# Products of a chunked recurrence grouped by the shape of their weights, and an order whose estimate counts changes of shape

## The chip, the cores and the metric

The kernel runs on one core of a Trainium2 chip. Its engines are TensorE (PE, with the weight loads listed apart as PEld), VectorE (DVE), ScalarE (ACT), GpSimd (POOL) and SyncE (SP, which only issues DMAs). The metric is the device time of one execution in microseconds, lower is better; the figure is the median of several executions.

## The reference

Two decoder layers and a final norm, for 256 prompt rows and 8 sample rows that share the weights. Each layer is a feed-forward half step, a mixer, and another feed-forward half step. The mixer of layer 0 joins a gated delta net (four heads) and differential attention (four heads); that of layer 1 is latent attention. The change touches the gated delta net of the prompt, which the reference computes in chunks of 64 rows:

```python
    def step(S, xs):
        q_i, k_i, u_i, w_i, a_i, gl = xs
        v_new = u_i - jnp.einsum('bhck,bhkv->bhcv', w_i, S)
        o = jnp.einsum('bhck,bhkv->bhcv', q_i, S) + jnp.einsum('bhij,bhjv->bhiv', a_i, v_new)
        S = S * jnp.exp(gl)[..., None, None] + jnp.einsum('bhck,bhcv->bhkv', k_i, v_new)
        return S, o
```

Here `u` and `w` are the solutions of a triangular system of each chunk, found before the scan. The eight samples make one step of the same recurrence each, from states of 256 KB that come from memory.

## The kernel before

All activations lie with features on the partitions and the 264 rows (prompt and samples together) as columns. A projection is a stream of 128 x 128 weight blocks: each block is split into a high and a low part (`whl`, by ACT and DVE), and three products of 264 columns use it. Small float32 products run as two passes, so a product of `mm` is two MATMUL records in the trace; the projection's products are one record each.

The program is written as threads (generators): `proj` is the mixer's input projection, `gdn` the recurrence of the prompt, `gdn_s` the step of the samples, `diff_p`, `diff_s` and `diff_v` the differential attention (`diff_s` multiplies the gathered keys `dk`, `diff_v` the gathered values `dv`), `post_d` and `post_g` the norms of the heads and the output projection (products on `mix`). A class `Clock` merges them into one queue for each engine: `emit` takes the instruction with the earliest estimated start, and `cost` holds the estimated durations. Nothing is reordered afterwards: the queues are fixed when the program is built, each engine works its own off in order, and the estimate only decides who stands before whom. A part written under `clk.group()` is placed as one piece. Where the estimate sees PE idle, `keep_warm` puts in products of a constant that nobody reads (`ps_pe<-busy`), so that the clock stays up; in the text they are called fillers.

What stands around the change in the mixer of layer 0:

- `gdn` inverts the triangular matrices by doubling (ten products `ps_pd<-ya` and `ps_pd<-yb,ya` of 64 x 64 blocks, sixteen at a time), transposes the keys, and then makes, for each half `b` of the heads' rows, `up` (weights of 64 rows and 64 columns) and `wpp` (weights of 64 rows and 128 columns), one product of each in turn.
- The scan has four chunks. A chunk makes `vp` from the state `SS`, on DVE the new values `vn`, then `sp` (the state's update) and `op_` (the output). `op_` of each head accumulates two products: one with the state as weights (128 rows), one with `vn` as weights (64 rows), again in turn.
- `gdn_s` waits for `proj`: the tiles `xh` and `xl`, which hold the projection's input, receive the samples' states. For four samples at a time it multiplies the states by keys and queries (`xh,gsw`, then `xl,gsw`), works on DVE, and adds the update (`gsr`).
- `post_g` waits for `gdn`, `gdn_s` and `proj`. So the first product on `mix` comes after the longer of the two recurrences and a head norm.

The accumulators are slots: `pa` two, `pc` one, `pd` three banks. `W.limit` holds the splitting of the output projection's weights back until `post_g` calls `W.resume()`.

Of the kernel before, what the change touches and what calls it, by code (L numbers as in the profile page):

```python
# [14 lines left out]
AF = mybir.ActivationFunctionType  # L15
# [127 lines left out]
class Virtual:  # L143
    """A tile whose place is chosen when its first instruction is put into a queue."""
# [5 lines left out]
class Slots:  # L150
    """Places of one shape for virtual tiles. The place of a tile is free again when its thread has gone past the
    segment that made it (keep: when the thread has called free) and its last instruction is in a queue."""
# [35 lines left out]
class Clock:  # L188
    """Puts the instructions that the threads create into the engine queues in the order of their
    estimated starts, so that no queue waits long at its head."""  # L190
# [5 lines left out]
    def __init__(self):  # L196
        self.free, self.reg, self.prev, self.rings = {}, {}, {}, {}
        self.pipe = self.hw = 0.0
        self.columns = {}
        self.spare = None  # L200
        self.seq = 0
        self.cur = self.atom = None
        self.waiting = {}
        self.done = {}
        self.virtual, self.segment = [None], []

    # -- tiles
# [48 lines left out]
    def when(self, r, write, eng=None):  # L256
        """When an instruction of `eng` may use the region."""
# [32 lines left out]
    # -- cost estimates  # L290
# [17 lines left out]
    def cost(self, eng, name, out, ins, k):  # L308
        n = max([self.size(out)] + [self.size(i) for i in ins]) if eng == "DVE" else self.size(out)
        if eng == "PE":  # L310
# [4 lines left out]
            if ins[0].dtype == F32R:  # L315
                return max(2.5 + n * 0.4167, m * 0.8333), n, share
# [21 lines left out]
    # -- instructions  # L338
# [82 lines left out]

    def start(self, eng, ri, ro):
        t = self.free.get(eng, 0.0)
        for r in ri:
            t = max(t, self.when(r, False, eng))
        for r in ro:
            t = max(t, self.when(r, True, eng))
        return t

    def pe(self, t, c, cols, share):  # L430
        """The tensor engine's clock is halved in each tick after one in which few columns left the array."""
# [6 lines left out]
    def keep_warm(self, t):  # L438
        """Matmuls that nobody reads, up to time t."""
        while self.spare:  # L440
# [3 lines left out]
            if f + c > t - self.MARGIN:  # L444
                return
            self.spare()
            self.free["PE"] = self.pe(f, 109.0, 256, 1.0)

    def emit(self, op):
# [3 lines left out]
        if eng == "PE":  # L453
            self.keep_warm(self.start(eng, op.calls[0][6], op.calls[0][7]))
        for f, name, a, k, out, ins, ri, ro in op.calls:
# [36 lines left out]
    def add(self, name):  # L492
        """What the current thread has created so far makes `name` available."""
# [6 lines left out]
    # -- threads: generators that yield None (go on when all that they issued is done), a time, or the  # L500
    # names they wait for
# [53 lines left out]
def hybrid_trunk_kernel(ctx: ExitStack, tc: tile.TileContext, wall, xT, wba, vecs, cst0, cst1, ident_d, convst,  # L555
# [29 lines left out]
    def service(thread, f, *a):  # L585
        """f's instructions in a thread of their own, which nobody waits for as a whole."""
        cur = clk.cur
        clk.cur = cur and thread
        f(*a)
        clk.cur = cur  # L590

    # ------------------------------------------------------------ weight stream
    class Stream:
        """The weights, 128 x 128 blocks in the order of their use; units of 16 blocks are loaded, pieces of 4 split into
        a high and a low part, except those that raw() hands out whole."""
# [54 lines left out]
        def whole(self, use):  # L650
            """use(the next block); with float32 products for these there is nothing to split."""
# [13 lines left out]
    # in the tensor engine's gaps it multiplies a constant, so that its clock stays up  # L665
# [17 lines left out]
    def rsqrt(src, w, np_=128):  # L683
        """1/sqrt of a small tile on the vector engine."""
# [17 lines left out]
    # ------------------------------------------------------------ constants  # L702
# [30 lines left out]
    # ------------------------------------------------------------ norm statistics  # L733
# [88 lines left out]
    # ------------------------------------------------------------ driver  # L822
# [21 lines left out]
    def lead(xh, xl, tags):  # L844
        """The first blocks of a projection; the last rows of x come latest, so the first two blocks alternate."""
# [17 lines left out]
    # ------------------------------------------------------------ FFN  # L863
# [58 lines left out]
    # ------------------------------------------------------------ final norm  # L922
# [18 lines left out]
    def finish_y():  # L941
        """The statistics with the tokens on the partitions; a product with their diagonal spreads them."""
# [21 lines left out]
    # ------------------------------------------------------------ KV gather  # L964
# [5 lines left out]
    class Loader:  # L970
        """Gathers tiles of 32-row strips of four pages each, in order, into whichever slots are free."""
# [40 lines left out]
        def retire(self, tags):  # L1012
            """These slots are not filled again."""
# [8 lines left out]
    # ------------------------------------------------------------ one sample's softmax over its past  # L1022
    def scores(b, w, load, parts, SM, ready, cc, P, pT):
        """w [128, sub, 32]: the queries, one diagonal block for each page of a strip; parts: for each part
        of the features, its four strips' tiles. Leaves exponentials (strip, page, query row; key) in P,
        transposed in pT; returns the inverses of their sums."""
# [30 lines left out]
    def weigh(o, pT, load, strips, vs, dv):  # L1057
        """o [32 j + query row, dv]: the values weighed by pT."""
# [13 lines left out]
    # ============================================================ start  # L1072
# [69 lines left out]
    # ============================================================ layer 0 mixer  # L1142
    def mixer0():
        with tc.tile_pool(name="m0", bufs=1) as mp_:
# [16 lines left out]
            # ---- input projection  # L1161
# [70 lines left out]
            # ---- normalisation of four head blocks by their partition sums  # L1232
# [13 lines left out]
            # ---- gated delta net  # L1246
# [19 lines left out]
            def gdn():  # L1266
# [59 lines left out]
                # decay in (key, query) layout, 64-token chunks stacked two high  # L1326
# [12 lines left out]
                # Gram products  # L1339
# [60 lines left out]
                # token-major keys and values  # L1400
                KB, KE = [], []
                for b in range(2):
# [7 lines left out]
                    yield  # L1410
                for b in range(2):
                    up, wpp = ps("pd"), (ps("pd"), ps("pd"))
                    for h in range(4):
                        for r in range(2):
                            rr = slice(r * 64, r * 64 + 64)
                            uc = U[rr, (4 * b + h) * 64:(4 * b + h) * 64 + 64]
                            hc = slice(h * 128, h * 128 + 128)
                            mm(up[rr, hc], uc, VB[b][rr, hc], start=True, stop=True)
                            mm(wpp[r][:, h * 64:h * 64 + 64], KB[b][rr, hc], uc, start=True, stop=True)
                    S.activation(VB[b], up, AF.Copy)  # L1420
                    for r in range(2):
                        S.activation(KB[b].rearrange("p (h r t) -> p h r t", h=4, r=2)[:, :, r, :],
                                     wpp[r][:, 0:256].rearrange("p (h t) -> p h t", h=4), AF.Copy)
                    yield
                # scan over the chunks
# [3 lines left out]
                for c in range(4):  # L1429
                    b, r = divmod(c, 2)  # L1430
                    rr = slice(r * 64, r * 64 + 64)
                    vp = ps("pd")
                    for h in range(4):
                        hc = slice(h * 128, h * 128 + 128)
                        mm(vp[rr, hc], KB[b][:, h * 128 + r * 64:h * 128 + r * 64 + 64], SS[:, h, :], start=True, stop=True)
                    V.tensor_tensor(vn[rr, :], VB[b][rr, :], vp[rr, :], OP.subtract)
                    yield
                    op_, sp = ps("pd"), ps("pd")
                    tc0 = b * 128 + r * 64
                    for h in range(4):  # L1440
                        hc = slice(h * 128, h * 128 + 128)
                        mm(sp[:, hc], KE[b][rr, hc], vn[rr, hc], start=True, stop=True)
                    for h in range(4):
                        hc = slice(h * 128, h * 128 + 128)
                        oc = slice(h * 64, h * 64 + 64)
                        mm(op_[:, oc], SS[:, h, :], Q0[:, h, tc0:tc0 + 64], start=True, stop=False)
                        mm(op_[:, oc], vn[rr, hc], AT[rr, (4 * b + h) * 64:(4 * b + h) * 64 + 64], start=False, stop=True)
                    V.tensor_tensor(SS, SS, egl[:, r, 4 * b:4 * b + 4, None].to_broadcast([128, 4, 128]), OP.mult)
                    V.tensor_tensor(SS, SS, v3(sp, 4), OP.add)
                    S.activation(Q0[:, :, tc0:tc0 + 64], op_[:, 0:256].rearrange("p (h t) -> p h t", h=4), AF.Copy)  # L1450
# [4 lines left out]
            # ---- gated delta net, one step of each sample: four samples at a time, row 32 j + 4 i + h  # L1455
# [758 lines left out]
```

## Time and profile before

| | before |
|---|---|
| median of 3 executions | 1348.65 us (1345.4 to 1349.91) |
| span of the profiled execution | 1297.2 us |
| median less the span | 51.45 us |
| PE busy, share of the span | 1274.9 us, 98% |
| mean granted clock of TensorE | 0.979 |
| input projection of the layer 0 mixer | 205.3 to 386.2 us |
| from its last product to the first on `mix` | 386.2 to 487.9 us |

The profile is of one execution; its own time outside the profiler is not given, so its span is set beside the median. PE counts as busy from the start of a product to its modelled end, and products overlap, so 98% does not mean that PE does useful work at its peak: half-speed products and fillers count too.

### The profile page before, as it was taken

Reading aid. Unit: us, or ns where it says so; the run is one execution under the profiler, and the core shown is the slowest. Engines: PE = TensorE matmul, PEld = TensorE weight load, DVE = VectorE, ACT = ScalarE, POOL = GpSimd, SP = SyncE. Lnnn points to the kernel's source line nnn. Section 1 sums busy time; section 2 is a strip of 40 time slices with the busy share of each in tenths; the row PEclk is TensorE's granted clock in tenths of the full one; section 3 lists DMA queues with packets and bytes.
Section 4 is the critical chain, followed back from the end, with each engine's and each line's share of the span. In section 5 each row is a group of like instructions: output and inputs, shape, how many; then the busy total and the mean of one; then the engine's idle time right before and its main releaser. Section 6 shows DMA issues by size and latency. Waiting matters only on the chain.

```text
span 1297.2 us, 28444 instructions
## 1 busy us (share of the span) xinstructions
PE 1274.9 (98%) x11569; PEld 1146.7 (88%) x11569; DVE 874.0 (67%) x1855; ACT 580.7 (45%) x1185; POOL 433.4 (33%) x526
## 2 busy tenths in 40 slices
PE   9999999999999999999999999999999999999997
PEld 7999999967676567999999999999876679999996
DVE  6777667687762767877766777766874449777652
ACT  5555544345411024555554555544432235555541
POOL 3643222355552412553422222212334523322221
PEclk9999999999996879999999999999999999999999
DMA  7776556898897563676755454555467955555551
GB/s 286 264 272 233 192 168 229 285 342 320 304 344 288 167 229 133 230 282 221 260 167 192 163 194 168 191 171 187 161 240 278 393 166 176 191 181 178 195 167 63
DMA packets 52163, 287.72 MB, mean 222 GB/s; under 512 B 6192, under 2 KB 6768, under 8 KB 27200
## 3 DMA queue, kind: packets, MB, share of 16 engines
q1 hardware_dynamic: 28912, 180.77, 40.0%
q0 software_dynamic: 23120, 105.13, 22.3%
q8 instruction: 91, 1.49, 0.4%
q14 instruction: 40, 0.33, 0.1%
HBM read 280.95 MB, written 5.03 MB: 220 GB/s over the span
## 4 chain that ended last, share of the span: by engine, by line
PE 86%; DVE 5%; DMA 3%; issue 2%; ACT 1%; POOL 1%; SPq 0%; POOLq 0%; ACTq 0%; DVEq 0%
PE ps_pd L457 40%; PE ps_pa L457 37%; PE ps_pc L457 5%; PE ps_po L457 3%; DVE whl L457 2%; PE ps_pe L666 2%; DMA dv<-in_vpool_dram,pt 2%; DMA raw<-in_wall_dram 1%; ACT whl L457 0%; DVE wxl L457 0%; DMA x<-in_xT_dram 0%; DVE QW L457 0%; DVE x L457 0%; POOL t L457 0%; DVE QR L457 0%
## 5 line engine op out<-in xcount | busy, mean ns | idle before, releaser
L457 DVE TENSOR_TENSOR whl<-raw,whl 128x512 fp32r<-128x512 f32 x642 | 486.0, 766 | 214.7 <-ACT whl L457 208.3
L457 ACT ACTIVATE whl<-raw 128x512 fp32r<-128x512 f32 x642 | 399.8, 630 | 371.9 <-PE ps_pa L457 195.9
L457 PE MATMUL ps_pa<-wxh,whl 128*128 128x264 f32 x1616 | 325.0, 286 | 1.8 <-ACT t L457 0.8
L457 PEld LDWEIGHTS ps_pa<-wxh,whl 128*128 128x128 f32 x1616 | 260.8, 188 | 11.0 <-issue 6.6
L457 PE MATMUL ps_pd<-wxh,whl 128*128 128x264 f32 x1152 | 233.9, 285 | 0.0
L457 PE MATMUL ps_pa<-wxl,whl 128*128 128x264 f32 x808 | 231.1, 286 | 0.0
L457 PEld LDWEIGHTS ps_pd<-wxh,whl 128*128 128x128 f32 x1152 | 187.6, 188 | 0.9 <-DVE whl L457 0.4
L457 POOL TENSOR_TENSOR t<-t,t 128x264 f32<-128x264 f32 (+1 forms) x100 | 83.1, 831 | 275.6 <-DVE t L457 275.4
L457 PE MATMUL ps_pd<-wxl,whl 128*128 128x264 f32 x576 | 164.1, 285 | 0.0
L457 PEld LDWEIGHTS ps_pa<-wxl,whl 128*128 128x128 f32 x808 | 151.8, 188 | 4.9 <-issue 4.5
L457 PE MATMUL ps_pd<-ah,whl 128*128 128x264 f32 x704 | 130.9, 284 | 0.0
L457 PE MATMUL ps_pa<-ah,whl 128*128 128x264 f32 x704 | 130.7, 284 | 0.0
L457 PEld LDWEIGHTS ps_pd<-ah,whl 128*128 128x128 f32 x704 | 110.0, 188 | 0.0
L457 PEld LDWEIGHTS ps_pa<-ah,whl 128*128 128x128 f32 x704 | 109.9, 188 | 0.0
L457 PEld LDWEIGHTS ps_pd<-wxl,whl 128*128 128x128 f32 x576 | 108.2, 188 | 0.8 <-issue 0.8
L457 PE MATMUL ps_pd<-al,whl 128*128 128x264 f32 x352 | 99.9, 284 | 0.0
L457 PE MATMUL ps_pa<-al,whl 128*128 128x264 f32 x352 | 99.7, 283 | 0.0
L457 POOL TENSOR_TENSOR al<-t,ah 128x264 fp32r<-128x264 f32 x88 | 76.9, 874 | 58.0 <-ACT ah L457 57.9
L457 POOL TENSOR_TENSOR t<-x 128x264 f32<-128x264 f32 x45 | 32.8, 730 | 189.0 <-DVE x L457 183.3
L457 POOL DMA_INDIRECT dk<-in_kpool_dram,ptk x57 | 58.8, 1031 | 56.9 <-PE ps_pc L457 45.2
L457 PE MATMUL ps_pd<-wya,whl 128*128 128x264 f32 x352 | 71.2, 284 | 0.0
L457 PE MATMUL ps_pa<-wya,whl 128*128 128x264 f32 x352 | 71.0, 284 | 0.0
(414 smaller groups left out, 1964.6 us busy)
## 6 DMA issues: line engine op xcount, KB each, us to landing
raw<-in_wall_dram SPq DMA_DIRECT2D x162, 1024.0 KB, 4.9
out_y_dram<-wya SPq DMA_DIRECT2D x4, 264.0 KB, 2.6
xh<-in_rec_dram SPq DMA_DIRECT2D x4, 256.0 KB, 9.5
xl<-in_rec_dram SPq DMA_DIRECT2D x4, 256.0 KB, 17.6
out_recs_dram<-xh SPq DMA_DIRECT2D x4, 256.0 KB, 7.1
out_recs_dram<-xl SPq DMA_DIRECT2D x4, 256.0 KB, 4.3
dk<-in_kpool_dram,ptk POOLq DMA_INDIRECT x57, 6.3
cst<-in_cst_dram SPq DMA_DIRECT2D x1, 838.5 KB, 8.7
```

Source lines behind the costliest of these rows:

```text
L457: f(*a, **k)
L666: clk.spare = lambda: nc.tensor.matmul(pe[0:32, 0:256], busy[:, 0:32], busy, start=True, stop=True)
```

## The change

Four edits. (1) `up` and `wpp` are two loops instead of one: for both halves all products of `up` first, then all of `wpp`, each half's eight in one group. (2) In a chunk of the scan the four products of one kind form a group: `vp`, then the output's part from the state, then `sp`, then the part from `vn`. The two parts of the output no longer accumulate in one bank: ACT copies the first to `Q0`, the second goes into the bank of `vp`, and DVE adds it (one more DVE instruction in each chunk). A chunk has one `yield` instead of two, and it asks for its three `pd` banks at once. (3) `emit` adds `SWITCH`, 120 ns, to the estimated time of PE where the shape of the weights (rows and columns, each rounded up to 32, 64 or 128) differs from that of the product before. (4) `cost` takes 121 ns instead of 112.5 for a projection product of 264 columns. Comments and docstrings are blanked as well.

```diff
-                return max(2.5 + n * 0.4167, m * 0.8333), n, share
+                return max(11.0 + n * 0.4167, 5.0 + m * 0.8333), n, share
...
+    SWITCH = 120.0
+    @staticmethod
+    def shape(call):
+        return tuple(32 if n <= 32 else 64 if n <= 64 else 128 for n in (call[5][0].shape[0], call[4].shape[0]))
...
             self.keep_warm(self.start(eng, op.calls[0][6], op.calls[0][7]))
+            kind = self.shape(op.calls[0])
+            if kind != self.kind and "PE" in self.free:
+                self.free["PE"] += self.SWITCH
+            self.kind = self.shape(op.calls[-1])
...
+                def both(b, f):
+                    with clk.group():
+                        for h in range(4):
+                            for r in range(2):
+                                rr = slice(r * 64, r * 64 + 64)
+                                f(h, r, rr, slice(h * 128, h * 128 + 128), U[rr, (4 * b + h) * 64:(4 * b + h) * 64 + 64])
...
-                            mm(up[rr, hc], uc, VB[b][rr, hc], start=True, stop=True)
-                            mm(wpp[r][:, h * 64:h * 64 + 64], KB[b][rr, hc], uc, start=True, stop=True)
+                    up = ps("pd")
+                    both(b, lambda h, r, rr, hc, uc: mm(up[rr, hc], uc, VB[b][rr, hc], start=True, stop=True))
                     S.activation(VB[b], up, AF.Copy)
+                for b in range(2):
+                    wpp = ps("pd"), ps("pd")
+                    both(b, lambda h, r, rr, hc, uc: mm(wpp[r][:, h * 64:h * 64 + 64], KB[b][rr, hc], uc, start=True, stop=True))
...
-                        mm(op_[:, oc], SS[:, h, :], Q0[:, h, tc0:tc0 + 64], start=True, stop=False)
-                        mm(op_[:, oc], vn[rr, hc], AT[rr, (4 * b + h) * 64:(4 * b + h) * 64 + 64], start=False, stop=True)
+                    with clk.group():
+                        for h, _, o in hs:
+                            mm(o, SS[:, h, :], Q0[:, h, tc0:tc0 + 64], start=True, stop=True)
                     V.tensor_tensor(vn[rr, :], VB[b][rr, :], vp[rr, :], OP.subtract)
+                    q = Q0[:, :, tc0:tc0 + 64]
+                    S.activation(q, op_[:, 0:256].rearrange("p (h t) -> p h t", h=4), AF.Copy)
                     V.tensor_tensor(SS, SS, egl[:, r, 4 * b:4 * b + 4, None].to_broadcast([128, 4, 128]), OP.mult)
+                    with clk.group():
+                        for _, hc, _ in hs:
+                            mm(sp[:, hc], KE[b][rr, hc], vn[rr, hc], start=True, stop=True)
                     V.tensor_tensor(SS, SS, v3(sp, 4), OP.add)
-                    S.activation(Q0[:, :, tc0:tc0 + 64], op_[:, 0:256].rearrange("p (h t) -> p h t", h=4), AF.Copy)
+                    with clk.group():
+                        for h, hc, _ in hs:
+                            mm(vp[:, h * 64:h * 64 + 64], vn[rr, hc], AT[rr, (4 * b + h) * 64:(4 * b + h) * 64 + 64], start=True, stop=True)
+                    V.tensor_tensor(q, q, vp[:, 0:256].rearrange("p (h t) -> p h t", h=4), OP.add)
```

The queues change in nearly every part of the program, since the estimate runs differently from the first product on. Three places on PE matter here. The first is the start of the first half's `up` (`yb 64x128`) and `wpp` (`yb,ya 128x64`) before; `dk,QW` are key products of the samples, and a shape is that of the result.

```order
L457 MATMUL ps_pc_71<-dk,QW 32x128 x24
L457 MATMUL ps_pd_73<-yb 64x128
L457 MATMUL ps_pd_72<-yb,ya 128x64
L457 MATMUL ps_pd_73<-yb 64x128
L457 MATMUL ps_pd_74<-yb,ya 128x64
L457 MATMUL ps_pd_73<-yb 64x128
L457 MATMUL ps_pd_72<-yb,ya 128x64
```

The pattern goes on for 16 products, and for 16 more of the second half. The same place now, with what follows it on PE:

```order
L470 MATMUL ps_pa_69<-wxl,whl 128x264
L470 MATMUL ps_pd_74<-yb 64x128 x8
L470 MATMUL ps_pd_72<-yb 64x128 x8
L470 MATMUL ps_pd_73<-yb,ya 128x64
L470 MATMUL ps_pd_74<-yb,ya 128x64
L470 MATMUL ps_pd_73<-yb,ya 128x64
L470 MATMUL ps_pd_74<-yb,ya 128x64
```

The sixteen products of `up` stand together, then those of `wpp`, which alternate between two banks, and products of the input projection (`wxl,whl`) now stand ahead of them. The second place is a chunk of the scan: before, the first chunk's `sp` (`yb,ya 128x128`) and `op_` (`S,SS` and `yb 128x64` in turn), with a group of the samples' queries between.

```order
L457 MATMUL ps_pd_72<-yb,ya 128x128 x4
L457 MATMUL ps_pd_73<-S_3172,SS 128x64
L457 MATMUL ps_pd_74<-xh,gsw 32x512 x4
L457 MATMUL ps_pd_73<-yb 128x64
L457 MATMUL ps_pd_73<-S_3172,SS 128x64
L457 MATMUL ps_pd_73<-yb 128x64
L457 MATMUL ps_pd_73<-S_3172,SS 128x64
```

Now, from the first chunk's `vp` (`SS,ya`) to the second chunk's `sp`:

```order
L470 MATMUL ps_pd_74<-SS,ya 64x128 x4
L470 MATMUL ps_pd_72<-S_3163,SS 128x64 x4
L470 MATMUL ps_po<-dv,PT_2540 8x512 x4
L470 MATMUL ps_pd_73<-yb,ya 128x128 x4
L470 MATMUL ps_pd_74<-yb 128x64 x4
L470 MATMUL ps_pa_69<-wxh,whl 128x264 x2
L470 MATMUL ps_pa_69<-wxl,whl 128x264
L470 MATMUL ps_pa_69<-wxh,whl 128x264
L470 MATMUL ps_pd_72<-SS,ya 64x128 x4
L470 MATMUL ps_pd_73<-S_3163,SS 128x64 x4
L470 MATMUL ps_pd_74<-yb,ya 128x128 x4
```

Each kind stands in fours, the step of the samples is gone from between, and the projection is still being fed: the scan, which stood wholly behind the projection's last product, now stands wholly ahead of it. The third place is what follows that last product. Before, the first of these rows stand right behind it: fillers, the first of the inverse's last two stages and the samples' first small product (`mfs,ones`):

```order
L666 LDWEIGHTS busy
L666 MATMUL ps_pe<-busy 32x256
L457 MATMUL ps_pd_74<-ya 64x64 x16
L666 LDWEIGHTS busy
L666 MATMUL ps_pe<-busy 32x256
L457 MATMUL ps_pd_73<-mfs,ones 128x64
```

Now, after 18 fillers, it is two value strips (`dv`) and the step of the samples, and behind `xh,gsw` come 39 fillers in a row:

```order
L470 MATMUL ps_po<-dv,PT_2538 8x512 x4
L470 MATMUL ps_pd_72<-mfs,ones 128x64
L470 MATMUL ps_po<-MX,PT_2538 8x128 x4
L470 MATMUL ps_po<-dv,PT_2538 8x512 x4
L679 LDWEIGHTS busy
L679 MATMUL ps_pe<-busy 32x256
```

```order
L470 MATMUL ps_pd_73<-ones,t_77 128x1 x2
L470 MATMUL ps_pd_74<-ident,gsw 128x128 x4
L470 MATMUL ps_pd_72<-ob,cst_104 32x128 x4
L470 MATMUL ps_pd_73<-xh,gsw 32x512 x4
L470 MATMUL ps_pd_72<-xh,gsw 32x512 x4
L679 LDWEIGHTS busy
```

Nothing of the prompt's recurrence is left behind the last projection product. In the whole program the fillers go from 317 to 398: while the input projection runs from 48 to 33, between its last product and the first on `mix` from 83 to 189, among the first products on `mix` from 23 to 35, elsewhere from 163 to 141.

## Rows read from the trace of the kernel before

**Rows 1.** The page: busy time, granted clock in 40 slices, the chain's shares.
```profile
PE 1274.9 (98%) x11569; PEld 1146.7 (88%) x11569; DVE 874.0 (67%) x1855; ACT 580.7 (45%) x1185; POOL 433.4 (33%) x526
...
PEclk9999999999996879999999999999999999999999
...
PE 86%; DVE 5%; DMA 3%; issue 2%; ACT 1%; POOL 1%; SPq 0%; POOLq 0%; ACTq 0%; DVEq 0%
```

**Rows 2.** Busy time by stage; at the end granted clock, DMA share, GB/s.
```profile
205.30:386.20 180.90, 177.22 (x2184) 141.08 (x2182) 132.78 (x369) 72.75 (x179) 81.91 (x118) 1.00 0.86 309
386.20:487.90 101.70, 100.32 (x835) 60.03 (x833) 53.98 (x154) 15.41 (x42) 28.21 (x30) 0.78 0.65 237
487.90:520.30 32.40, 31.65 (x249) 26.49 (x248) 26.20 (x62) 13.86 (x27) 9.32 (x11) 1.00 0.32 113
520.30:909.30 389.00, 388.47 (x3181) 386.23 (x3180) 275.41 (x465) 203.31 (x373) 120.22 (x135) 1.00 0.58 202
```

**Rows 3.** PE in order of time around the projection's end: start, duration, instruction.
```profile
386.09 0.28 PE L457 MATMUL ps_pa<-wxh,whl 128*128 128x264 f32 x1
...
386.73 1.15 PE L457 MATMUL ps_pd<-ya 64*64 64x64 f32 x32
...
388.43 0.61 PE L666 MATMUL ps_pe<-busy 128*32 128x256 bf16 x4
...
391.21 1.04 PE L457 MATMUL ps_po<-dv,PT 128*8 128x512 f32 x8 [1.09 <-DMA dv<-in_vpool_dram,pt]
392.19 0.66 PE L457 MATMUL ps_pd<-ident,S 128*128 128x128 f32 x4
```

**Rows 4.** The same view, from 395 us: `up` and `wpp` in turn.
```profile
395.93 1.52 PE L457 MATMUL ps_pc<-dk,QW 128*32 128x128 f32 x48
397.38 0.43 PE L457 MATMUL ps_pd<-yb 64*64 64x128 f32 x2
397.74 0.43 PE L457 MATMUL ps_pd<-yb,ya 64*128 64x64 f32 x2
...
404.77 2.36 PE L457 MATMUL ps_pc<-dk,QW 128*32 128x128 f32 x40
407.06 0.69 PE L457 MATMUL ps_pd<-yb 64*64 64x128 f32 x2
...
416.88 1.51 PE L457 MATMUL ps_pc<-dk,QW 128*32 128x128 f32 x24
418.15 1.08 PE L457 MATMUL ps_pd<-xh,gsw 128*32 128x512 f32 x4
```

**Rows 5.** A stretch within these, columns as in group 2.
```profile
400.80:421.30 20.50, 20.50 (x124) 13.18 (x124) 0.91 (x3) 2.51 (x6) 4.29 (x5) 0.50 0.59 221
```

**Rows 6.** PE in order of time, the scan's last chunk.
```profile
462.23 1.16 PE L457 MATMUL ps_pd<-yb,ya 64*128 64x128 f32 x8
463.31 0.43 PE L457 MATMUL ps_pd<-S,SS 128*128 128x64 f32 x2
463.68 0.43 PE L457 MATMUL ps_pd<-yb 64*128 64x64 f32 x2
...
466.60 1.93 PE L457 MATMUL ps_pc<-dk,QW 128*32 128x128 f32 x32
```

**Rows 7.** Instructions on `xh`, 380 to 460 us: the last line.
```profile
DMA to landing us min/median/max: 7.0/7.4/11.2
```

**Rows 8.** DVE in order of time: the samples' step, the scan's end, the norm.
```profile
425.64 1.51 DVE L457 SCALAR_TENSOR_TENSOR t<-ps_pd,ghe,t 128x128 f32<-128x128 f32 x4 [2.06 <-PE ps_pd L457]
...
435.94 0.17 DVE L457 COPY S<-ps_pd 128x16 f32<-128x16 f32 x1
...
457.98 0.17 DVE L457 COPY S<-ps_pd 128x16 f32<-128x16 f32 x1 [0.66 <-PE ps_pd L457]
...
466.81 0.69 DVE L457 TENSOR_TENSOR SS<-SS,ps_pd 128x512 f32<-128x512 f32 x1
```

**Rows 9.** PE in order of time: the first products on `mix`.
```profile
487.92 0.39 PE L457 MATMUL ps_pa<-mix,whl 128*128 128x264 f32 x1
```

More of the change, by code (lines that the diff above doesn't have):

```diff
@@ L202, in __init__ @@
         self.cur = self.atom = None
+        self.kind = None
         self.waiting = {}
@@ L445, in keep_warm @@
                 return
+            self.kind = (128, 32)
             self.spare()
@@ L1410, in gdn @@
                     yield
-                for b in range(2):
[L1412 to L1417, printed above, removed]
-                            mm(up[rr, hc], uc, VB[b][rr, hc], start=True, stop=True)
-                            mm(wpp[r][:, h * 64:h * 64 + 64], KB[b][rr, hc], uc, start=True, stop=True)
+                def both(b, f):
[4 more added lines that the diff above has]
+                                f(h, r, rr, slice(h * 128, h * 128 + 128), U[rr, (4 * b + h) * 64:(4 * b + h) * 64 + 64])
+                for b in range(2):
+                    up = ps("pd")
+                    both(b, lambda h, r, rr, hc, uc: mm(up[rr, hc], uc, VB[b][rr, hc], start=True, stop=True))
                     S.activation(VB[b], up, AF.Copy)
+                for b in range(2):
+                    wpp = ps("pd"), ps("pd")
+                    both(b, lambda h, r, rr, hc, uc: mm(wpp[r][:, h * 64:h * 64 + 64], KB[b][rr, hc], uc, start=True, stop=True))
                     for r in range(2):
@@ L1423, in gdn @@
                                      wpp[r][:, 0:256].rearrange("p (h t) -> p h t", h=4), AF.Copy)
-                    yield
+                yield
                 LK.retire(f"whl{i}" for i in range(N_SPL))
@@ L1431, in gdn @@
                     rr = slice(r * 64, r * 64 + 64)
[L1432 to L1435, printed above, removed]
-                    V.tensor_tensor(vn[rr, :], VB[b][rr, :], vp[rr, :], OP.subtract)
-                    yield
-                    op_, sp = ps("pd"), ps("pd")
-                    tc0 = b * 128 + r * 64
@@ L1440, in gdn @@
[L1440 to L1445, printed above, removed]
-                        mm(op_[:, oc], SS[:, h, :], Q0[:, h, tc0:tc0 + 64], start=True, stop=False)
-                        mm(op_[:, oc], vn[rr, hc], AT[rr, (4 * b + h) * 64:(4 * b + h) * 64 + 64], start=False, stop=True)
+                    vp, op_, sp = ps("pd"), ps("pd"), ps("pd")
@@ new lines, in gdn @@
+                    tc0 = b * 128 + r * 64
+                    hs = [(h, slice(h * 128, h * 128 + 128), op_[:, h * 64:h * 64 + 64]) for h in range(4)]
+                    with clk.group():
+                        for h, hc, _ in hs:
+                            mm(vp[rr, hc], KB[b][:, h * 128 + r * 64:h * 128 + r * 64 + 64], SS[:, h, :], start=True, stop=True)
+                    with clk.group():
+                        for h, _, o in hs:
+                            mm(o, SS[:, h, :], Q0[:, h, tc0:tc0 + 64], start=True, stop=True)
@@ L1449, in gdn @@
                     V.tensor_tensor(SS, SS, v3(sp, 4), OP.add)
-                    S.activation(Q0[:, :, tc0:tc0 + 64], op_[:, 0:256].rearrange("p (h t) -> p h t", h=4), AF.Copy)
+                    with clk.group():
+                        for h, hc, _ in hs:
+                            mm(vp[:, h * 64:h * 64 + 64], vn[rr, hc], AT[rr, (4 * b + h) * 64:(4 * b + h) * 64 + 64], start=True, stop=True)
+                    V.tensor_tensor(q, q, vp[:, 0:256].rearrange("p (h t) -> p h t", h=4), OP.add)
```

## The prediction

> **What bounds the kernel now.** I read the page first, then the busy time by stage, then PE in order of time around the recurrence, then DVE there. The page [rows 1] shows PE busy 98% of the span and on 86% of the chain that ended last; its clock row falls below 9 only in slices 13 to 15, 400 to 490 us. In the plain stretches PE is truly full: two feed-forward halves take 389.0 us for 3181 products, 0.122 us each [rows 2]. The order can't change that. The stage that the change can move is the mixer of layer 0: 180.9 us while the input projection runs, 101.7 us from its last product to the first on `mix`, 32.4 us for the output projection [rows 2]. Of the middle one PE is "busy" 100.3 us, at a mean clock of 0.78 [rows 2], which means that about 45 us of it ran at 1.2 instead of 2.4 GHz. So before the change PE sets the pace there too, but with slow work: the reader sees it in [rows 4], where `up` and `wpp` take turns. One product takes 0.36 us (397.38 to 397.74) and, from 400.8 us on, where the clock is halved for 20.5 us [rows 5], about 0.61. The 32 products take 7.4 us and 9.8 us [rows 4], 17.2 us in all, while DVE is busy 0.9 us in 20.5 [rows 5]. Behind them stands the scan, whose `op_` takes turns likewise: 3.3 us for eight products in the last chunk, against 1.08 us for the four of `sp`, which keep one shape [rows 6].
>
> **The change, part by part.** The sum is made in the profiled execution: its last projection product starts at 386.1 us [rows 3], its first on `mix` at 487.9 [rows 9]. Its span is 51.45 us below the median shown; I take a difference in the span as one in the median.
>
> *Grouped `up` and `wpp`.* No row shows exactly these in a group. The nearest is a stage of the inverse, which also has weights of 64 rows and alternates between the two halves of the partitions: 16 products in 1.15 us, 0.07 each [rows 3]; but its products have half the columns or half the weights. The upper end is `sp`, which stays in one half: 0.27 each [rows 6]. So 32 products cost 2.3 to 8.6 us; they are nearer to the inverse (they alternate), twice its work, and I take 4. That is 13 less than measured, 7.5 less than the 11.5 that they would take at full clock.
>
> *Grouped scan.* A chunk becomes four groups of four. `sp` itself is the row: 1.08 us [rows 6]. The state's group has full weights and 64 columns, that of `vn` has the weights of `sp` and fewer columns, so both are priced like it: 4.3 us a chunk, 17.3 in all; upper end, if grouping gains nothing: the two kinds of `op_` cost 3.3 us a chunk as in turns now and not 2 x 1.08, 4.6 more in all, 21.9.
> The Trainium skill, "TensorE: Matmul & The Clock Gate", in the section on packing small matmuls, says that a weight load overlaps products in flight only where the row group differs. All four products of `sp` use the same 64 rows, and yet follow each other at 0.27 us, faster than today's turns at 0.36 [rows 6]; the row speaks against the rule here. By the rule the two kinds of `op_` would gain nothing, and the sum would come out at its upper end of 21.9, 4.6 us later.
>
> *The added DVE instruction*, `q` plus the bank of `vp`, works on half of the columns of the update of `SS`, which takes 0.69 us [rows 8]; four times that is under 2.8 us. The next chunk needs `SS` and not `Q0`, so it lies beside the next `vp`; only `gdn_s` and the norm stand behind, and both now start later. I cost it at nothing; uncovered it is 0.7 us. A chunk now holds all three `pd` banks; what queues for them are the products on `ob` and the norm of `post_d`, which nobody waits for before the projection's end.
>
> *What moves ahead of the last projection product.* By the order of the two programs: 128 products of keys (24 in the 1.45 us from 395.93 to 397.38, 0.06 each [rows 4]): 7.7 us. 32 products of values, eight groups of 0.98 us [rows 3]: 7.8. Two stages of the inverse: 2.3. Two groups of key transposes at 0.66 [rows 3]: 1.3. `up` and `wpp`: 4. The scan: 17.3. Thirty small products of the samples' score ends, of `ob`, `MX` and one head norm, each between 0.06 and 0.36 us [rows 4]: 2 to 11, I take 5. Less 15 fillers at 0.11 us (four in 0.61, of which the last product's end is 0.28 [rows 3]): -1.7. Sum 43.7. So the projection ends near 429.8 us instead of 386.1, if PE stays fed. What has to come for it is eight strips of values more, 1 MB each, 190 GB/s over that time; the stage behind the projection moved 237 GB/s [rows 2], so I add nothing, but PE did wait 1.09 us for such a strip [rows 3].
>
> *What is left behind it.* Now the step of the samples alone, and it is a chain, not work of PE: (a) the states land 7.0 to 11.2 us after their issue [rows 7]: 10. (b) Four samples: from the keys' products over DVE's work to the copy of the result. The second half of it, from 425.64 to 435.94, took 10.3 us, of which about 4 were the scan's and the scores' instructions in DVE's queue [rows 8]; with the part ahead of it, two groups of 1.1 us and six DVE instructions of 0.3 to 0.4, I take 11. (c) The other four: 11. (d) From the recurrence's end to the first product on `mix`: 487.92 less 467.5 [rows 8, 9] is 20.4 us, in which two head norms shared DVE; one of them is now done earlier: 18. Sum 50 us. From below it is bounded by PE's own queue there: 189 fillers at 0.11 and some 20 us of products, 41. From above by the steps as they ran before: 11.2, then 17.8 from the first product of the samples at 418.15 [rows 4] to the copy at 435.94, 22.0 to the next copy at 457.98 [rows 8], and 20.4: 71. I stay near the lower end because what stood between these steps (turns of `op_`, values, keys) is gone.
>
> *The first product on `mix`* so comes at 429.8 + 50 = 479.8 instead of 487.9: 8.1 us earlier. Twelve more fillers follow among the first of them (+1.3), and two groups of values and one of `ob` no longer do (-2.4): 1.1. Elsewhere 22 fillers fewer, which stood between full projection products: 2 us. Sum 11.2 us; 1348.65 less 11 is 1337.5, and I say 1338.
>
> **The rivals.**
> *Faster still.* The clock stays up through the recurrence (the 45 us at half clock would be 22 shorter at full clock if PE alone set the pace in them; as an estimate 17) and the chain (a) to (d) runs near PE's queue, 43 us: 429.8 - 2 + 43 = 471, with the 3 elsewhere 20 us, 1329. For it: fillers now fill the tail. Against: DVE's chain isn't shortened by them.
> *No change: the clock falls in the scan.* The grouped scan is 20 us of small products with four projection products between, and before, 3.4 us after the turns began, the clock halved [rows 4, 5]. A halved clock raised a product from 0.36 to 0.61 us; over the scan and `up`/`wpp`, 21.3 x 0.7 = 15 us if it lasts through, 7 if through half: 1345 to 1352.
> *Slower: the step of the samples lies bare.* Before, its waits were covered by the scan's products; now only fillers stand there. If each step keeps its old length, the tail is 71 us, the first product on `mix` comes at 501, and the whole takes 1359. It decides from a tail of 65 us on (11 + 4 above 50).
>
> **How the numbers follow.** A measurement of this kernel can tell about 0.3%, 4 us, from no change. Forecast (1331 to 1344.5): 0.48. Faster still (1322 to 1331): 0.20. No change (1344.6 to 1352.7): 0.17. Slower: 0.15. So faster 0.68, same 0.17, slower 0.15. The range leaves out one in ten on either side: 1324 to 1355.
>
> **What would show it.** Right: in the changed profile `up` and `wpp` stand as two blocks of under 3 us each; groups of four in the scan near 1.1 us; the last projection product between 425 and 436 us; PE full of fillers behind it, DVE's chain of the samples at 10 to 12 us for four, and the first product on `mix` between 474 and 486. Wrong: a clock row that falls during the scan; PE waits for `dv` ahead of the projection's end; or a tail above 60 us with DVE or the states' DMA as the releaser. The prediction is wrong, too, if the two feed-forward halves behind the mixer (389.0 us [rows 2]) move by more than 3 us.

## The result and the profile after

The changed kernel takes 1361.05 us (1360.19 to 1362.64, 4 runs) against 1349.28 before: a ratio of 1.0102, 95% interval 1.0077 to 1.0127. It is 1% slower; 1338 was forecast. The page of the profile after, for [rows 1]:

```profile
PE 1290.3 (95%) x11650; PEld 1160.7 (85%) x11650; DVE 875.7 (64%) x1859; ACT 578.8 (43%) x1185; POOL 432.3 (32%) x526
...
PEclk9999999898998988999999999999998989999999
...
PE 81%; DVE 8%; issue 4%; DMA 2%; ACT 2%; another core or an unknown queue 2%; POOL 1%; POOLq 0%; ACTq 0%; DVEq 0%
```

PE's share falls from 98 to 95%, DVE and "issue" (waits with no releaser) grow on the chain, and the dips of the clock row start at slice 8 instead of 13. Busy time by stage of the changed kernel, columns as in [rows 2], from the layer 0 projection to the end of the layer 1 mixer:

```profile
204.57:478.44 273.87, 243.96 (x2808) 185.10 (x2806) 161.13 (x435) 79.58 (x199) 97.16 (x135) 0.92 0.71 253
478.44:531.52 53.08, 44.95 (x337) 26.21 (x335) 35.80 (x110) 9.25 (x25) 12.27 (x13) 0.84 0.57 211
531.52:562.84 31.32, 30.41 (x228) 26.81 (x228) 24.82 (x46) 13.37 (x25) 9.68 (x11) 1.00 0.33 106
562.84:951.40 388.56, 387.97 (x3176) 385.85 (x3177) 267.06 (x464) 200.72 (x373) 120.55 (x135) 1.00 0.58 202
951.40:1123.20 171.80, 152.56 (x1623) 115.09 (x1622) 86.90 (x284) 52.17 (x146) 60.17 (x69) 0.94 0.62 220
```

The last projection product starts at 478.44 us, not at 429.8. The next stretch takes 53.1 us, near the 50 forecast. A difference of 93 us in the projection against [rows 2] can't be right beside a measured 12: this span is 2 us under the time of its own execution (1361.63), that of before was 51 under its median. So the first experiment profiled the kernel before once more. Its stages:

```profile
205.04:419.96 214.92, 196.58 (x2185) 153.27 (x2183) 132.45 (x369) 72.47 (x179) 83.14 (x121) 0.93 0.77 274
419.96:520.25 100.29, 98.23 (x835) 59.45 (x835) 53.59 (x154) 15.41 (x42) 25.10 (x26) 0.80 0.60 213
520.25:552.98 32.73, 31.78 (x249) 26.52 (x249) 26.55 (x63) 13.98 (x28) 9.66 (x11) 1.00 0.32 107
552.98:941.29 388.31, 388.22 (x3179) 386.11 (x3179) 273.02 (x464) 203.23 (x373) 121.77 (x135) 1.00 0.58 203
941.29:1105.31 164.02, 152.03 (x1636) 114.20 (x1634) 86.35 (x284) 51.70 (x146) 58.61 (x69) 0.97 0.64 231
```

The same program takes 214.9 us for the projection here and 180.9 in [rows 2]; the stretch behind it is the same (100.3, 101.7). In the projection PE is idle 18.3 us (length less busy) and about 30 us at half clock (twice the length times one less the granted clock); in [rows 2] 3.7 and none. The layer 1 mixer differs too, 164.0 us here and 151.2 in the first profile. This profile's span, 1342.1, fits its execution (1343.99), and in the projection of all 14 further profiles PE is idle 18 us or more as well. It is the base from here on.

| us | projection | to first on `mix` | to last on `mix` | mixer 1 | sum |
|---|---|---|---|---|---|
| before, profiled again | 214.9 | 100.3 | 32.2 | 164.0 | 511.4 |
| changed | 273.9 | 53.1 | 30.8 | 171.8 | 529.6 |
| difference | +59.0 | -47.2 | -1.4 | +7.8 | +18.2 |
| forecast | +43.7 | -51.8 | -1.1 | 0 | -9.2 |

(With 2 us elsewhere the forecast came to -11.2.) The feed-forward stages agree within 0.6 us. The spans differ by 17.3 us, the medians by 11.8; this execution of before was 5 us under the median that stands beside the changed kernel.

What the change was to do to the products it did. PE in order of time, the changed kernel, for [rows 4, 6]:

```profile
441.37 2.55 PE L470 MATMUL ps_pd<-yb 64*64 64x128 f32 x32
443.86 1.11 PE L470 MATMUL ps_pd<-yb,ya 64*128 64x64 f32 x16
...
445.21 1.34 PE L470 MATMUL ps_pd<-yb,ya 64*128 64x64 f32 x16
...
447.45 1.09 PE L470 MATMUL ps_pd<-SS,ya 128*64 128x128 f32 x8
448.47 1.10 PE L470 MATMUL ps_pd<-S,SS 128*128 128x64 f32 x8
...
450.48 1.16 PE L470 MATMUL ps_pd<-yb,ya 64*128 64x128 f32 x8
451.48 1.00 PE L470 MATMUL ps_pd<-yb 64*128 64x64 f32 x8
```

`up` is one block of 2.5 us, its first part still at half clock (0.50 granted from 441.4 to 442.4 us), `wpp` two of 1.1 to 1.3, and each group of the scan about 1.1 us. And the stretch behind the projection is a chain with little under it. PE in order of time there:

```profile
478.65 2.14 PE L679 MATMUL ps_pe<-busy 128*32 128x256 bf16 x18
...
485.58 1.04 PE L470 MATMUL ps_po<-dv,PT 128*8 128x512 f32 x8 [2.34 <-DMA dv<-in_vpool_dram,pt]
...
488.88 2.85 PE L470 MATMUL ps_pd<-xh,gsw 128*32 128x512 f32 x15
...
491.58 4.09 PE L679 MATMUL ps_pe<-busy 128*32 128x256 bf16 x36
...
520.11 7.11 PE L679 MATMUL ps_pe<-busy 128*32 128x256 bf16 x59
527.15 0.34 PE L470 MATMUL ps_pd<-ident,AO 128*128 128x128 f32 x1
...
531.52 0.39 PE L470 MATMUL ps_pa<-mix,whl 128*128 128x264 f32 x1
```

and DVE's ends of the two groups of four samples, with the head norm's input:

```profile
501.17 0.17 DVE L470 COPY S<-ps_pd 128x16 f32<-128x16 f32 x1
...
516.80 0.17 DVE L470 COPY S<-ps_pd 128x16 f32<-128x16 f32 x1 [0.19 <-PE ps_pd L470]
...
523.79 0.29 DVE L470 TENSOR_SCALAR AO<-AO,rsy 128x128 f32<-128x128 f32 x1
```

Steps (a) to (d) of the prediction read off: 10.4 us to the first state product (488.88), 12.3 to the first copy (501.17), 15.6 to the second (516.80), 14.7 to `mix`. The filler rows stand for PE with nothing to do. They can also be in the way: `AO` is ready at 524.1, and its product runs at 527.15, behind 59 of them. What the other fillers cost was not tried in a run.

### The profile page after: what moved, and what is told of

Read it like the earlier page. It is cut to its first block, busy times and chain, and to the rows that moved or that the text cites. A ratio compares the mean times of both kernels' runs of the same rounds, so it can differ in the third digit from the quotient of the medians.

```text
span 1359.4 us, 28606 instructions
## 1 busy us (share of the span) xinstructions
PE 1290.3 (95%) x11650; PEld 1160.7 (85%) x11650; DVE 875.7 (64%) x1859; ACT 578.8 (43%) x1185; POOL 432.3 (32%) x526
## 4 chain that ended last, share of the span: by engine, by line
PE 81%; DVE 8%; issue 4%; DMA 2%; ACT 2%; another core or an unknown queue 2%; POOL 1%; POOLq 0%; ACTq 0%; DVEq 0%
PE ps_pd L470 37%; PE ps_pa L470 34%; PE ps_pc L470 5%; PE ps_po L470 3%; PE ps_pe L679 2%; DVE whl L470 2%; DVE t L470 2%; DMA raw<-in_wall_dram 2%; DMA dv<-in_vpool_dram,pt 1%; ACT whl L470 1%; DVE dps L470 0%; DVE wxl L470 0%; DVE rsa L470 0%; DVE x L470 0%
## 5 line engine op out<-in xcount | busy, mean ns | idle before, releaser
L470 PE MATMUL ps_pa<-wxh,whl 128*128 128x264 f32 x1616 | 329.9, 289 | 3.7 <-DVE t L470 3.3
L470 PEld LDWEIGHTS ps_pa<-wxh,whl 128*128 128x128 f32 x1616 | 265.6, 192 | 10.3 <-issue 5.8
L470 PE MATMUL ps_pa<-wxl,whl 128*128 128x264 f32 x808 | 234.0, 290 | 0.0
L470 POOL TENSOR_TENSOR t<-t,t 128x264 f32<-128x264 f32 (+1 forms) x100 | 87.0, 870 | 292.3 <-DVE t L470 290.0
L470 PEld LDWEIGHTS ps_pa<-wxl,whl 128*128 128x128 f32 x808 | 154.6, 191 | 6.6 <-issue 5.7
L470 POOL TENSOR_TENSOR t<-x 128x264 f32<-128x264 f32 x45 | 32.2, 717 | 188.6 <-DVE x L470 183.0
L470 POOL TENSOR_TENSOR al<-t,ah 128x264 fp32r<-128x264 f32 x88 | 70.8, 805 | 49.1 <-ACT ah L470 49.1
```

The source lines that it names most:

```text
L470: f(*a, **k)
```

## Experiments

All were run beside the kernel before on the same chip; ratios are against it, with 95% intervals. The median of before went from 1344.95 to 1349.49 us between the groups of runs, so between groups the ratios compare better than the times. The table behind the last one has the stages.

**The kernel before, again**, with no edit.

> The kernel before, unchanged, with a profile. Its first profile has a span of 1297.2 us, 51 us under its median, while the changed kernel's span of 1359.4 is 2 us under the time of the same execution. Theory A (the first profile of before shows an execution unlike the timed ones): the new profile has a span of 1343 to 1348 us, TensorE waits in the layer 0 projection as it does in the changed kernel, and that projection ends at 410 us or later. Theory B (51 us lie outside the span of before): the span is 1295 to 1300 us again, and the projection's last product starts at 386 us.

1343.99 us, span 1342.1: theory A, with the span 0.9 us below its range. PE's waits there, 204.5 to 420 us, by what ended them:

```profile
PE ps_pd L457 <- issue: 5.4, 6, 2.0
PE ps_pc L457 <- issue: 4.0, 9, 1.0
PE ps_pd L457 <- ACT whl L457: 2.7, 1, 2.7
PE ps_pa L457 <- issue: 1.6, 3, 0.9
```

The same view of the first profile has no line with "issue".

**One part at a time.** Groups without the new estimate; the estimate with the old products; the change without SWITCH:

```diff
# groups only
-    SWITCH = 120.0
+    SWITCH = 0.0
-                return max(11.0 + n * 0.4167, 5.0 + m * 0.8333), n, share
+                return max(2.5 + n * 0.4167, m * 0.8333), n, share
# estimate only: before.py with edits (3) and (4)
# no switch
-    SWITCH = 120.0
+    SWITCH = 0.0
```

> The grouped products with the old estimate (SWITCH 0, 112.5 ns a projection product): inverse, up, wpp and scan stand behind the projection's last product, as before. Theory A (the new order costs, the groups gain): faster than before by 8 to 14 us, 1335 to 1341 us, up and wpp two or three blocks of under 3 us each. Theory C (the groups themselves cost, by their wait for three banks or by an idle engine and a lower clock): as slow as the changed kernel, 1356 to 1364 us.

> The old products in turn, with the new estimate (SWITCH 120 ns and the longer projection product): the scan stands ahead of the projection's last product, as in the changed kernel. Theory A (the order costs): slower than before by 20 us or more, 1369 to 1380, that is the changed kernel plus what the groups gain. Theory C (the groups cost): 1345 to 1352, as before.

> The changed kernel with SWITCH 0, the longer projection product kept: scan, up and wpp stand behind the projection's last product. Theory A: the switch's 120 ns are what moves the scan, so 1335 to 1343 us, near the groups alone. Theory C: 1356 to 1364 us. If the longer projection product is what costs (elsewhere, in the feed-forward halves), it is above the groups alone by 5 us or more.

Measured: groups only 1337.26 us (0.994, 0.9923 to 0.9956); estimate only 1388.37 (1.0321, 1.0297 to 1.0345); no SWITCH 1331.06 (0.9897, 0.9879 to 0.9915). Theory A in each, with sizes beyond it twice (the estimate alone is 8 us slower, the change without SWITCH 4 us faster than it allowed). The groups gain 0.6%, the longer projection product 0.4% more, and SWITCH turns a gain of 1.0% into a loss of 1.0%. The stages without SWITCH:

```profile
205.02:423.65 218.63, 195.81 (x2185) 151.20 (x2184) 133.01 (x370) 72.71 (x179) 83.93 (x121) 0.92 0.76 275
423.65:502.74 79.09, 71.45 (x759) 43.36 (x757) 55.65 (x157) 15.75 (x42) 24.71 (x26) 0.87 0.65 235
```

The projection is 55 us shorter than with SWITCH, the stretch behind it only 26 longer. `up` and `wpp` in the groups-only kernel, where the granted clock is 1.00 throughout:

```profile
427.67 1.96 PE L470 MATMUL ps_pd<-yb 64*64 64x128 f32 x32
429.56 1.11 PE L470 MATMUL ps_pd<-yb,ya 64*128 64x64 f32 x16
...
430.95 1.30 PE L470 MATMUL ps_pd<-yb,ya 64*128 64x64 f32 x16
```

They take 4.2 us by their starts, against the 11.5 us of turns at full clock in the prediction. Three of the turns in the second profile of before:

```profile
432.48 0.43 PE L457 MATMUL ps_pd<-yb 64*64 64x128 f32 x2
432.84 0.43 PE L457 MATMUL ps_pd<-yb,ya 64*128 64x64 f32 x2
433.20 0.43 PE L457 MATMUL ps_pd<-yb 64*64 64x128 f32 x2
```

**Where SWITCH costs.** The scan held behind the projection; SWITCH in mixer 0 (and what stands before it) only; everywhere but there; and, without SWITCH, the scan as before:

```diff
# scan behind
+                yield from wait("proj")
                 def both(b, f):
# SWITCH in mixer 0 only
+    clk.SWITCH = 0.0
     mixer1()
# SWITCH not in mixer 0
+    clk.SWITCH = 0.0
     mixer0()
+    clk.SWITCH = 120.0
# up and wpp only: SWITCH 0, the scan's loop of before.py
```

> The changed kernel, SWITCH 120 ns kept, but the recurrence waits for the projection ahead of up, so that up, wpp and the scan (with 64 key and 4 value products) stand behind the projection's last product again. Theory A (the scan's place ahead of the projection's end is what costs): 1335 to 1345 us, the projection's last product below 455 us against 478.4, the tail 65 to 80 us. Theory D (the other orders that SWITCH makes inside the projection cost): 1352 us or more.

> The changed kernel with SWITCH set to 0 from the mixer of layer 1 on. That mixer took 171.8 us in the changed kernel's profile and 163.5 to 165.5 in those with SWITCH 0 or without it. Theory E (SWITCH costs some 8 us there too): 1351 to 1355 us. Rival (those 8 us are the profile's execution, or follow from what ran before): 1358 to 1363.

> The complement: SWITCH 0 in the mixer of layer 0 alone, 120 ns elsewhere. Theory A with E: mixer 0 as in the kernel without SWITCH (1331.1), plus the 8 us in mixer 1, so 1337 to 1341. Rival of E: 1329 to 1333. If mixer 0 isn't where SWITCH costs: 1350 or more.

> SWITCH 0, the longer projection product, up and wpp grouped, the scan as before in turns. By the prediction's terms (13 us for up and wpp, 4.6 for the scan) it keeps most of the gain: 1333 to 1338 us, against 1331.1 with both. If the scan's grouping is worth more, because its products and the samples' step end the tail: 1340 to 1346.

Measured: scan behind 1351.01 (1.0022, 1.0001 to 1.0043); mixer 0 only 1354.11 (1.0043, 1.0022 to 1.0063); not in mixer 0 1337.25 (0.9927, 0.9901 to 0.9953); up and wpp only 1336.95 (0.9922, 0.9894 to 0.995). Theory E holds both ways: SWITCH costs 4 to 8 us in mixer 1 and about 20 to 24 in mixer 0. The first is between the theories: holding the scan back regains 10 of the 30 us (by the ratios 11 of 28). Theory A's range didn't yet count the 4 to 8 us of mixer 1, which this kernel still pays; in the three stages of mixer 0 it regains 12.7 of 23.1 us. Its projection still takes 241.5 us, 22.9 more than without SWITCH, while what stands ahead of its end in addition (64 key products, four groups of values, a stage of the inverse, 16 fillers) is worth 10.6 by the prediction's prices; 5.5 us more idle time and 13 us more at half clock, about 7, make up the rest. The last, within the first of its ranges, shows that the scan's groups are worth 3 (by the ratios) to 6 us of the whole.

**How much SWITCH, where counted, and the bursts of key products.**

```diff
# SWITCH 40, SWITCH 80
-    SWITCH = 120.0
+    SWITCH = 40.0
# small shapes: SWITCH 120
-            if kind != self.kind and "PE" in self.free:
+            if kind != self.kind and (128, 128) not in (kind, self.kind) and "PE" in self.free:
# thinned keys: SWITCH 0, behind the four products of every second step
+                    if s % 2:
+                        mm(pe[0:32, 0:256], busy[:, 0:32], busy, start=True, stop=True)
```

> The changed kernel with SWITCH 40 ns: the scan, all 128 late key products and two stages of the inverse stand behind the projection's last product, as before. Theory A (the cost hangs on what the order moves ahead): 1329 to 1337 us. Theory D (the cost grows with the length that SWITCH adds to the estimate): a third of the way from 1331 to 1361, so 1339 to 1343.

> The changed kernel with SWITCH 80 ns: the same work as with 120 stands ahead of the projection's last product. Theory A: 1355 to 1363 us, a step against 40 ns. Theory D: two thirds of the way, 1349 to 1353.

> The changed kernel, SWITCH 120 ns counted only where neither the product before nor the next has weights of 128 x 128, so that leaving or entering the projection's stream costs nothing in the estimate. The scan stands behind the projection. Theory A: 1329 to 1337 us. Theory D (any added length costs): 1340 or more.

> SWITCH 0 with the longer projection product, and in the bursts of key products one filler (0.11 us) after every 16 of them. If PE's waits for no releaser in the bursts come from the rate at which its short instructions are supplied, these waits fall from 16 in the kernel without fillers there to 5 or fewer, the clock stays up, and the time is at or under 1331 us in spite of some 10 us of fillers. If they don't depend on the rate: as many waits, and 1336 to 1343 us.

Measured: 40 ns 1345.46 (1.0007, 0.9987 to 1.0027); 80 ns 1361.76 (1.0148, 1.0115 to 1.0181); small shapes 1327.52 (0.987, 0.9857 to 0.9882); thinned 1341.32 (0.9974, 0.9962 to 0.9987). In mixer 0 theory A holds: its three stages take 335.3 us with 40 ns and 355.1 with 80, against 334.7 and 357.8 with 0 and 120, a step where the scan changes sides. The time at 40 ns lies above the ranges of both theories all the same: mixer 1 already pays in full (172.2 us), and the profiled execution was 4 us under the median. The projection with 80 ns:

```profile
205.23:477.34 272.11, 239.42 (x2816) 181.61 (x2815) 159.07 (x431) 80.71 (x199) 94.18 (x134) 0.95 0.70 253
```

Counted between small shapes alone, the same 120 ns cost nothing in either mixer (1.5 us below theory A's range). This version beats both kernels, by 1.3% and 2.3%. The fillers in the bursts, one after every 16 records (eight products), didn't take the waits away: the view of PE's waits has 19 with no releaser at `ps_pc`, and 20 without these fillers. In the projection 17 us run at half clock, for 35 without them; groups only has 17 as well, so it isn't shown that the fillers did it. Mixer 1 takes 14 us more.

**Is the stretch behind the projection the samples' step?** The second four samples left out, in the changed kernel and in the small-shapes version:

```diff
-                for t in range(2):
+                for t in range(1):
                     r4 = recs[4 * t:4 * t + 4]
```

> The changed kernel with the samples' step for four samples only: the states' products, DVE's work and the stores of the other four are left out. Theory F (the stretch from the projection's last product to the first on mix is the samples' step laid bare, and PE only fills): that stretch falls from 53.1 us by the whole step (c), 11 to 16 us, to 37 to 42, and the time from 1361 to 1345 to 1350 us. Rival (the stretch is bound by the value strips, the last head norms or PE's own queue): it falls by under 5 us, 1356 us or more.

> The same left out of the kernel in which SWITCH counts only between small shapes (1327.5 us, scan and key products behind the projection's last product). Theory F: there the step lies beside other work of PE, so only its products go, some 4 us, and the stretch falls by 2 to 6 us: 1321 to 1326 us. Rival (the step is bare there too): it falls by 11 us or more, to 1317 or less.

Measured: 1344.97 (0.9995, 0.998 to 1.001) and 1321.71 (0.9816, 0.9789 to 0.9843). The changed kernel loses 16.1 us, the other 5.8 (by the ratios 14 and 7). The stretch in the changed kernel without the four samples; then in the small-shapes version with all, and without four:

```profile
476.47:512.12 35.65, 29.57 (x242) 16.71 (x240) 24.01 (x75) 8.26 (x21) 8.36 (x9) 0.90 0.77 283
```

```profile
422.87:503.14 80.27, 70.56 (x792) 42.26 (x791) 54.91 (x159) 15.44 (x42) 25.76 (x26) 0.91 0.68 253
```

```profile
426.85:498.93 72.08, 65.35 (x794) 42.24 (x792) 48.88 (x142) 15.57 (x41) 20.85 (x22) 0.95 0.71 267
```

It falls by 17.4 us where the step is bare (53.1 to 35.7), which is its step (c) of 15.6 and more, and by 8.2 where other work lies beside it: theory F, though both falls are 1 to 2 us more than it allowed. (In the second pair the projection is 5 us longer without the four samples, so projection and stretch together fall by 3 us only.)

| profile, us | projection | to first on `mix` | to last on `mix` | mixer 1 | fillers, mixer 0 | ratio |
|---|---|---|---|---|---|---|
| groups only | 211.6 | 85.5 | 38.3 | 165.5 | 144 | 0.994 |
| estimate only | 295.3 | 54.5 | 30.8 | 170.6 | 282 | 1.0321 |
| no SWITCH | 218.6 | 79.1 | 37.0 | 163.5 | 110 | 0.9897 |
| scan behind | 241.5 | 70.6 | 33.0 | 168.9 | 133 | 1.0022 |
| mixer 0 only | 275.3 | 52.0 | 30.8 | 163.4 | 257 | 1.0043 |
| not in mixer 0 | 217.8 | 81.4 | 35.1 | 170.0 | 105 | 0.9927 |
| up and wpp only | 218.3 | 82.2 | 33.2 | 167.9 | 118 | 0.9922 |
| SWITCH 40 | 218.5 | 85.3 | 31.5 | 172.2 | 144 | 1.0007 |
| SWITCH 80 | 272.1 | 52.2 | 30.8 | 170.7 | 282 | 1.0148 |
| small shapes | 216.6 | 80.3 | 31.1 | 162.3 | 121 | 0.987 |
| thinned keys | 215.9 | 80.7 | 32.7 | 177.2 | 162 | 0.9974 |
| changed | 273.9 | 53.1 | 30.8 | 171.8 | 257 | 1.0102 |

The fillers are counted in the order of the programs.

## Why the prediction was wrong

From the first projection product to the end of mixer 1 the forecast was -9.2 us and the profiles have +18.2 (the medians of the whole +11.8). Of these 27.4 us, 15.3 lie in the projection, 4.6 in the stretch behind it, 7.8 in mixer 1; the products on `mix` give back 0.3.

*The groups: right in sum.* `up` and `wpp` were to fall from 17.2 us to 4; by the starts of their products they fell from 16.4 in the second profile of before to 4.8. The scan was to take 17.3 and takes 15.9 (21.9 before). So 17.6 us of PE's time are gone, as the terms said; that 11.6 and 6.0 add up to the same as 13.2 and 4.6 is luck. In the whole kernel the groups bring only 0.6%, 8 us (groups only). The rule of the Trainium skill ("TensorE: Matmul & The Clock Gate", on packing small matmuls), by which the two kinds of `op_` would not gain, isn't borne out there: they went from 11.9 us to 7.9. Nor is it in the feed-forward halves, where weight loads that fill all rows are busy 385.85 of 388.56 us beside products busy 387.97. Yet the half of the rows does count, which the prediction left out. Two blocks of one shape (`64*128 64x64`) stand in the changed kernel: 16 records of `wpp`, which alternate between the two halves of the rows, take 1.11 us, and eight of the scan, which keep one half, 1.00. That isn't the alternating banks of `wpp`: `up` alternates its halves in one bank, and 32 records take 1.96 us. In the turns of before the half changes from each `wpp` to the next `up`, and the step takes 0.36 us (432.84 to 433.20) as it does where the half stays (432.48 to 432.84). So here alternating halves helped only together with a kept shape.

*The stretch behind the projection: right.* 53.1 us for 50, by the chain named. Step (c) was too short (15.6 for 11), (d) too long (14.7 for 18), so part of the agreement is luck. The rival *the clock falls in the scan* didn't come: the granted clock is 1.00 from 443.9 to 478 us.

*"So the projection ends near 429.8 us instead of 386.1, if PE stays fed": this step failed.* It priced the moved work and put idle time and clock at nothing. The move cost 59.0 us, not 43.7: in the projection of the changed kernel PE is busy 47.4 us longer and idle 11.6 us longer (29.9 for 18.3). Some 44 us run at half clock for 30, which costs about 7 of the 47.4; so the work itself took about 40, no more than its price, and what failed is "if PE stays fed". With SWITCH 80, which moves the same work, it is 42.8 us more busy and 14.4 more idle. The condition was taken for granted because the one profile read had PE idle for 3.7 us; in all others it is idle 18 to 26 us before anything is moved, so some of the 11.6 may be this spread. Which waits come from the moved work and which from its neighbours wasn't separated: the longest is 4.7 us for `ya` between stages of the inverse, and the smaller move (scan behind) already brings 28.3 us of idle time.

*The balance around it.* The sum subtracted 51.8 us behind the projection and didn't ask what that time was. Without SWITCH the scan and the keys lie beside the samples' step, and the step costs little, as leaving out half of it shows (5.8 us). With SWITCH nothing of the prompt lies beside it (16.1 us for the same four samples), and PE spends the time on fillers: 147 more in mixer 0 than without SWITCH, at 0.11 us 16 of the 23 us by which mixer 0 is longer. The work that had covered the step went where PE was full already. That is the mechanism of the rival "the samples' step lies bare", but it was tied to a tail of 65 us; with the projection as it is, 53 are enough.

*"Elsewhere 22 fillers fewer: 2 us", and nothing in mixer 1: wrong.* Its order did change with SWITCH, and it costs 4 to 8 us there. Which of its orders does it is open.

*The base.* A difference in spans was taken as one in medians, from a profile whose span lay 51 us below. The distance was named, but not read as a sign that this execution had waited less than the timed ones. Over its span PE was idle 22 us less than in the second profile and 31 us less at half clock (mean granted clock 0.979 and 0.968). Why is open.

## What to carry to other kernels

Grouping products by the shape of their weights was worth a factor of 2.8 in PE's time where the products also alternate between two halves of the rows (11.5 us at full clock to 4.2), and of 1.5 where they keep one half or fill all rows (11.9 to 7.9). It doesn't need the planner to know of shapes. A price put into a planner's estimate reorders everything that shares it: before pricing work that moves, ask what it covered where it stood, and whether the engine has room where it goes. And where a profile's span lies far from the medians, profile again before any term is taken from it.

## What the runs showed of the hardware

PE waits in the midst of bursts of small products, with no releaser. PE in order of time in the changed kernel:

```profile
390.75 1.39 PE L470 MATMUL ps_pc<-dk,QW 128*32 128x128 f32 x44
392.40 0.44 PE L470 MATMUL ps_pc<-dk,QW 128*32 128x128 f32 x4 [0.27 <-issue]
393.16 0.43 PE L470 MATMUL ps_pc<-dk,QW 128*32 128x128 f32 x5 [0.32 <-issue]
393.91 0.43 PE L470 MATMUL ps_pc<-dk,QW 128*32 128x128 f32 x5 [0.33 <-issue]
394.63 0.38 PE L470 MATMUL ps_pc<-dk,QW 128*32 128x128 f32 x2 [0.29 <-issue]
```

Forty-four records run at 0.03 us each, then four or five at a time, 0.75 us apart, at a granted clock of 1.00 throughout. The view of PE's waits has no wait of this kind for the first profile of before and 12 to 24 at `ps_pc` for each of the 15 others. Of 269 ahead of products on `QW` in these 15, 160 (59%) end within 2.5 us of the start of a 16 KB packet of the instruction queue (q8), where the packets' spacing would give 37% by chance; the waits stand in clusters, so there are fewer independent cases than that. This speaks for the supply of instructions. Against it, the first profile has the same 91 packets and no such wait, and a quarter more time in the bursts (thinned keys) hardly lessened them. So the cause isn't shown.
